# Longer runs of tile-sized matmuls in a decoder step's sparse attention: scores, values, pooling and compressed values

## The chip, the cores and the metric

The kernel runs on one core of a Trainium2 chip. The metric is the device time of one execution in microseconds (us); lower is better. Kernels are compared by the median of repeated runs on the same chip.

## The reference

One step of a one-layer hybrid decoder, for 256 prompt tokens and 8 sample sequences of 8 tokens (320 token rows in all), model width 2048, all in float32:

```python
h = rmsnorm(x); u = h @ w_in            # 2048 x 23664, columns shared out among the mixers
y = x + (sigmoid(m_A) * (GDN(u) @ w_branch_a) + sigmoid(m_B) * (NSA(u) @ w_branch_b)) @ w_out
```

GDN is a gated delta rule (32 heads of 128). NSA is sparse attention with 16 query heads over 4 key heads, and three branches that are added with gates:

- **compressed**: keys and values of 32 tokens, every 16 tokens, are pooled with learned weights and mapped by a 128x128 matrix; softmax over the 127 pooled blocks of a sequence, and a score that picks 16 blocks of 64 tokens.
- **selected**: attention over the picked blocks of the sequence's 2048 cached tokens (16 pages of 128 tokens, found through a page table), and the 8 new tokens. The kernel reads all 16 pages and masks what was not picked.
- **window**: attention over the last 512 cached tokens and the new ones.

The prompt has the same three branches over its own 256 tokens. Besides y, the step returns the new caches and states.

## The kernel before

The program is written out flat: Python code emits every instruction once, and each engine runs its list in that order. The order is not written by hand. The parts of the layer are generators ("streams"). Before each step a stream yields the engine it wants, and the buffers that have to be ready; `Run.go` takes the stream whose next step could start first by a planner (`Clock`, with assumed durations), lets it emit that step, and goes on. So what stands in the code as one step (between two yields) is emitted without other work in between; a yield is a place where other streams' work can come between. The projection (`p_load`, `p_hi`, `p_lo`, `p_mm`) has the lowest rank on TensorE and fills what the others leave.

**The projection.** `p_load` brings slabs of w_in (later w_branch_a, w_branch_b, w_out) of up to 1 MB into three buffers `wraw`. ScalarE rounds 128x512 pieces to `whi`, VectorE makes the remainder `wlo`, and TensorE multiplies each 128x128 block three times into `acc` (128x320): `hhi,whi`, `hlo,whi`, `hhi,wlo`. One 1 MB slab is 48 such matmuls, the whole layer 11,952 of them. Everything that the mixers need comes out of this, so the delta rule's work can only be reached in step with it.

**The attention streams**, which the change edits:

- `pooled` and `compressed` (lines 1158 to 1233): per sequence and per key or value, 16 pages of 128x512 through a `Feed` of 6 buffers `cpg`. Per step four pages are pooled by four matmuls with 32 weight columns each (`Pk`), which write partitions 0, 32, 64, 96 of `pp`. Then transposes, the 128x128 mapping, softmax, ranking (`select`).
- `scores` (line 1291): for each page, four 128x128 transposes into PSUM (`nt`), a copy to SBUF (`kT`, on ScalarE and VectorE in turn), and four matmuls of 32 columns, one per key head, into a quarter of `ns` each. `e.nt` pages go together: one in the window, two in the selected branch. The new tokens' scores (`kS`) follow at the end of each sequence as four 32x64 matmuls.
- `weighted` (line 1333): the softmax rows `x` are transposed four blocks at a time into `pT`, and each page of values gives four 32x128 matmuls into `op`, `e.nt` pages to a step; the new tokens' values (`vS`, 64 rows) are last.
- `prompt` (line 997): per key head and half of the tokens, four heads; the compressed probabilities are transposed as four 64-column blocks, and their values are a matmul with 64 rows (`vcp`) after the full ones in the same `op`.
- `window` runs beside `prompt` over the cached window with 5 page buffers `wpg`. When both are done, two `sample` workers (4 sequences each, 10 page buffers `spg` each) run the selected branch; the delta rule follows.

A float32 matmul is two matmuls in the trace (fp32 goes through twice); transposes and the fp32r matmuls of the projection are one. "Tile work" below means matmuls that use a part of the 128x128 array: 32 or 64 columns or rows. Pages go through the one queue of SyncE (SP), in the order of the program, with the weight slabs. For a page of `k_sel` or `v_sel` SP reads its number from a register; `page` (line 1129) keeps the numbers of a sequence in registers, and loads them again (`ptab`) when another sequence has taken the place.

Of the kernel before, what the change touches and what calls it, by code (L numbers as in the profile page):

```python
# [10 lines left out]
F32 = mybir.dt.float32  # L11
F32R = mybir.dt.float32r
I32 = mybir.dt.int32
AF = mybir.ActivationFunctionType
# [7 lines left out]
P = 128  # L22
# [20 lines left out]
NWP = 5  # L43
# [392 lines left out]
def step(ctx: ExitStack, tc: tile.TileContext, I, O):  # L436
# [395 lines left out]
    vcp = wtab.tile([64, 4, P], F32, name="vcp")  # L832
# [131 lines left out]
    def prompt_compress(tok):  # L964
        V.memset(kcpT, 0.0)
        V.memset(vcp, 0.0)
        for kv, nm in enumerate(("kc", "vc")):
            yield ("pe", tok[nm], Next(wps, "a"))
            pp = wps.tile([P, 512], F32, tag="a", name="pp")
            for t in range(2):  # L970
                T.matmul(pp[:32], Pk[:, kv, t], tok[nm][:, t], start=t == 0, stop=t == 1)
            yield "dve"
            pl = wk.tile([32, 512], F32, tag="wpcT", name="pl")
            V.tensor_tensor(pl.rearrange("p (g d) -> p g d", g=4), pp[:32].rearrange("p (g d) -> p g d", g=4),
                            bc(cb[:32, kv], [[0, 4], [1, P]]), op=OP.add)
            yield ("pe", clock.last, Next(wps, "b"))
            tp = wps.tile([P, 512], F32, tag="b", name="tp")
            for g in range(4):
                T.transpose(tp[:, g * 32:g * 32 + 32], pl[:, g * P:g * P + P], ident[:32, :32])
            yield "dve"  # L980
            pt = wprep.tile([P, P], F32, tag="pt", name="pt")
            V.tensor_copy(pt, tp[:, :P])
            yield ("pe", clock.last, Next(wps, "b"))
            if kv == 0:
                kp = wps.tile([P, 512], F32, tag="b", name="kp")
                T.matmul(kp[:, :P], proj[:, 0], pt, start=True, stop=True)
                rs = yield from rstd(wprep, wps, "a", kp[:, :P], P, None)
                V.scalar_tensor_tensor(kcpT[:, :, :32], kp[:, :P].rearrange("p (g n) -> p g n", g=4), gains[:, 1:2],
                                       rs.rearrange("p (g n) -> p g n", g=4), op0=OP.mult, op1=OP.mult)
            else:  # L990
                vp = wps.tile([P, 512], F32, tag="b", name="vp")
                for g in range(4):
                    T.matmul(vp[:32, g * P:g * P + P], pt[:, g * 32:g * 32 + 32], proj[:, 1], start=True, stop=True)
                yield "dve"
                V.tensor_copy(vcp[:32].rearrange("p g d -> p (g d)"), vp[:32])

    def prompt():
        yield lambda: done["names"]
        qp = {}
        for g, tt in ((g, tt) for g in range(4) for tt in range(2)):  # L1000
# [35 lines left out]
            pcT = wk.tile([64, 512], F32, tag="wpcT", name="pcT")  # L1036
            S.activation(pcT, tp[:64], AF.Copy)
            ob = wk.tile([P, 4, P], F32, tag="wob", name="ob")
            for h in range(4):
# [38 lines left out]
                T.matmul(op[:, :P], vcp[:, g], pcT[:, h * P:h * P + P], start=False, stop=True)  # L1078
# [73 lines left out]
    cfeed = Feed(cp, "cpg", 6, [page(key, b, 4 * j + i) for b in range(B) for key in ("k_cmp", "v_cmp")  # L1152
                                for i in range(4) for j in range(4)], CR)

    def qT(b, g):
        return qs[:, b, 4 * g:4 * g + 4, :].rearrange("p h t -> p (h t)")

    def pooled(b, kv):
        pp = cps.tile([P, 512], F32, tag="a", name="pp")
        for i in range(4):  # L1160
            pg = []
            for _ in range(4):
                pg.append((yield from cfeed.get()))
            yield ("pe", *pg)
            for j in range(4):
# [4 lines left out]
            cfeed.release(4)  # L1170
# [66 lines left out]
    def select(h):  # L1237
# [17 lines left out]
        for a in (0, 15):  # L1255
            big = cp.tile([P, 2, 450], F32, tag="big", name="big", bufs=1)
            mine, other = bc(sc[:, a:], [[1, 15], [0, 30]]), bc(sc, [[0, 15], [1, 30]])
            v = [big[:, k].rearrange("p (a b) -> p a b", a=15) for k in range(2)]
# [13 lines left out]
    class Env:  # L1272


        def __init__(self, pp, st, tt, nt, pl, n, i, feed):
            self.feed, self.next, self.nt = feed, Next(pp, tt), nt
            self.s = lambda name: pp.tile([P, 512], F32, tag=st, name=name)
            self.t = lambda name: pp.tile([P, 512], F32, tag=tt, name=name, bufs=nt)
            self.x = lambda name: pl.tile([P, 512], F32, tag=f"{name}{i}", name=name, bufs=n)
# [11 lines left out]
    def scores(e, b, npg, dst, kS, finish):  # L1291

        for quad in range(0, npg, 4):
            ns = e.s("ns")
            prev = []
            for p in range(0, 4 + e.nt, e.nt):
                got, now = [], []
                if p < 4:
                    for _ in range(e.nt):
                        got.append((yield from e.feed.get()))  # L1300
                    yield ("pe", *got, e.next)
                    for k, pg in enumerate(got):
                        if k:
                            yield ("pe", e.next)
                        nt = e.t("nt")
                        for g in range(4):
                            T.transpose(nt[:, g * P:g * P + P], pg[:, g * P:g * P + P], ident)
                        now.append(nt)
                        e.feed.release()
                if prev:  # L1310
                    yield ("pe", *prev)
                    for k, kT in enumerate(prev):
                        for g in range(4):
                            T.matmul(ns[32 * g:32 * g + 32, (p - e.nt + k) * P:(p - e.nt + k + 1) * P], qT(b, g), kT[:, g * P:g * P + P], start=True, stop=True)
                prev = []
                for k, nt in enumerate(now):
                    prev.append(e.x("kT"))
                    if (p + k) % 2:
                        yield ("dve", nt)
                        V.tensor_copy(prev[k], nt)  # L1320
                    else:
                        yield ("act", nt)
                        S.activation(prev[k], nt, AF.Copy)
            yield ("dve", ns)
            finish(quad, ns)
        yield ("pe",)
        ns = e.s("ns")
        for g in range(4):
            T.matmul(ns[32 * g:32 * g + 32, :64], qT(b, g), kS[:, g], start=True, stop=True)
        yield "dve"  # L1330
        V.scalar_tensor_tensor(dst[:, npg * P:npg * P + 64], ns[:, :64], SCALE, newB[:, 56 - 8 * b:120 - 8 * b], op0=OP.mult, op1=OP.add)

    def weighted(e, b, npg, x, vS, op):
        prev = None
        for quad in list(range(0, npg + 1, 4)) + [None]:
# [8 lines left out]
            if prev is not None:  # L1344
                q0, n0, m0, pT = prev
                for k in range(0, n0, e.nt):
                    got = []
                    for _ in range(min(e.nt, n0 - k)):
                        got.append((yield from e.feed.get()) if q0 < npg else vS)
                    yield ("pe", *got, pT)  # L1350
                    for i, pg in enumerate(got):
                        c = (k + i) * P
                        for g in range(4):
                            T.matmul(op[32 * g:32 * g + 32], pT[:m0, c + 32 * g:c + 32 * g + 32], pg[:m0, g * P:g * P + P],
                                     start=q0 == 0 and k + i == 0, stop=q0 == npg)
                        if q0 < npg:
                            e.feed.release()
            if quad is not None:
                pT = e.x("pT")
# [6 lines left out]
                prev = quad, n, m, pT  # L1366

    def window():
        for b in range(B):
# [7 lines left out]
            yield from scores(wenv, b, 4, xw, kwS, fin_w)  # L1377
            yield from softmax(xw, 576, b, 2, mx)
            op = wenv.s("op")
# [20 lines left out]
    wenv = Env(wps, "a", "b", 1, wwin, 1, "", Feed(wwin, "wpg", NWP, [wpage(key, b, p) for b in range(B) for key in ("k_win", "v_win") for p in range(4)]))  # L1400
# [8 lines left out]
    def sample(smp, sps, n, bs):  # L1409
        req = [page(key, b, p) for b in bs for key in ("k_sel", "v_sel") for p in range(16)]  # L1410
        env = Env(sps, "s", "t", 2, smp, 2, "", Feed(smp, "spg", n, req))
        for b in bs:
# [16 lines left out]
            yield from scores(env, b, 16, xs, ksS, fin_s)  # L1429
# [3 lines left out]
            op = sps.tile([P, 512], F32, tag="s", name="op")  # L1433
# [905 lines left out]
```

## Time and profile before

| | |
|---|---|
| median of 3 runs | 2661.42 us (2658.48 to 2663.15) |
| the profiled execution's own time | 2657.93 us |
| its span, first to last instruction | 2655.9 us |
| TensorE matmul busy | 2581.8 us (97%), 22228 instructions |
| TensorE weight load busy | 2332.5 us (88%) |
| VectorE, ScalarE, GpSimd busy | 62%, 53%, 15% |
| HBM traffic over the span | 203 GB/s |
| mean granted TensorE clock | 0.988 |

What lies around the span is 2.0 us. In the profile PE is TensorE's matmuls and PEld its weight loads, DVE is VectorE, ACT ScalarE, POOL GpSimd, SPq the queue of SyncE. A row of the timeline gives the start, the time from the first start to the last end, and how many equal matmuls were merged. Matmuls overlap, so the distance from one start to the next is what a matmul costs, not its duration. All operations go through one recording helper, so the line is L330 nearly everywhere and the tile names tell them apart: `acc` is the projection, `pp` pooling, `nt` a transpose of a page or of softmax rows, `ns` scores, `op` values, `ps`, `pu` and `bank` the delta rule.

In time the program is: norms and the first weights, pooling beside the projection (84 to 858 us), prompt and window (438 to 811 us), the selected branch (818 to 1107 us), the delta rule's state beside the projection (1322 to 2222 us), and the projections out to the end.

### The profile page before, as it was taken

To read this page: it belongs to the slowest core of one execution; us is meant where nothing else is said; L and a number is where in the kernel's file an instruction comes from. 1 tells how busy PE (TensorE), PEld (TensorE's weight loads), DVE (VectorE), ACT (ScalarE), POOL (GpSimd) and SP (SyncE) were. 2 spreads that over 40 slices of the span, in tenths; PEclk is the share of its full clock that TensorE was granted. 3 is DMA by queue.
4 is the path that set the end of the run, shared out by engine and by line. 5 is a ranking of instruction groups with operands and counts; after the bars stand their busy time and mean duration, and the time that the engine had idled before them with its cause. 6 is when DMAs were issued, how large, how long until landed. Compare 5 with 4: busy or idle time off the path is not lost. (4 is left out here: it accounts for less than half of the span.)

```text
span 2655.9 us, 59457 instructions
## 1 busy us (share of the span) xinstructions
PE 2581.8 (97%) x22228; PEld 2332.5 (88%) x22228; DVE 1648.4 (62%) x4089; ACT 1407.7 (53%) x3290; POOL 398.0 (15%) x967
## 2 busy tenths in 40 slices
PE   7999999999999999999999899989999899999999
PEld 5897788777878888899999699979998789999999
DVE  5554445655556555544887787878878776454543
ACT  5453443434433333345778568777777565444443
POOL 2000011000000000000222343324242322000000
PEclk9999999999999999999999899989999899999999
DMA  6747777898768998765546256545464366656654
GB/s 193 232 156 242 232 238 268 273 322 267 252 207 281 316 359 273 242 195 156 153 152 189 88 179 180 163 131 154 145 189 147 122 195 216 208 180 191 184 191 131
DMA packets 548677, 543.89 MB, mean 205 GB/s; under 512 B 32482, under 2 KB 452499, under 8 KB 548003
## 3 DMA queue, kind: packets, MB, share of 16 engines
q1 hardware_dynamic: 534308, 493.67, 58.3%
q0 software_dynamic: 14080, 46.41, 5.1%
q8 instruction: 175, 2.87, 0.4%
q14 instruction: 114, 0.93, 0.1%
HBM read 470.31 MB, written 69.67 MB: 203 GB/s over the span
## 5 line engine op out<-in xcount | busy, mean ns | idle before, releaser
L330 PE MATMUL acc<-hhi,whi 128*128 128x320 f32 (+1 forms) x3472 | 1146.3, 330 | 1.5 <-ACT hhi L330 1.5
L330 PE MATMUL acc<-hhi,wlo 128*128 128x320 f32 (+1 forms) x3472 | 1075.3, 310 | 0.0
L330 PE MATMUL acc<-hlo,whi 128*128 128x320 f32 (+1 forms) x3472 | 1074.1, 309 | 0.5 <-DVE hlo L330 0.4
L330 ACT ACTIVATE whi<-wraw 128x512 fp32r<-128x512 f32 (+1 forms) x996 | 626.2, 630 | 834.5 <-PE acc L330 792.4
L330 DVE TENSOR_TENSOR wlo<-wraw,whi 128x512 fp32r<-128x512 f32 x992 | 685.4, 694 | 576.3 <-ACT whi L330 545.6
L330 PEld LDWEIGHTS acc<-hhi,whi 128*128 128x128 f32 (+1 forms) x3472 | 654.9, 189 | 70.1 <-issue 57.4
L330 PEld LDWEIGHTS acc<-hlo,whi 128*128 128x128 f32 (+1 forms) x3472 | 655.6, 189 | 7.0 <-issue 2.2
L330 PEld LDWEIGHTS acc<-hhi,wlo 128*128 128x128 f32 (+1 forms) x3472 | 653.5, 188 | 0.0
L330 PE MATMUL acc<-oah,whi 128*128 128x320 f32 x512 | 158.2, 309 | 0.0
L330 PE MATMUL acc<-oal,whi 128*128 128x320 f32 x512 | 158.2, 309 | 0.0
L330 PE MATMUL acc<-oah,wlo 128*128 128x320 f32 x512 | 158.2, 309 | 0.0
L330 POOL CAST vx<-v 32x128 fp32r<-32x128 f32 x256 | 97.8, 382 | 143.7 <-DVE v L330 91.5
L298 POOL DMA_DIRECT2D d_mz<-raw x48 | 26.2, 545 | 605.5 <-ACT raw L330 594.1
L330 DVE SCALAR_TENSOR_TENSOR cv<-xp,cw,cv 128x344 f32<-128x344 f32 x192 | 109.9, 573 | 6.0 <-ACT cv L330 4.7
L330 ACT ACTIVATE kT<-nt 128x512 f32<-128x512 f32 x80 | 47.6, 596 | 109.2 <-PE ns L330 63.4
L330 DVE COPY kT<-nt 128x512 f32<-128x512 f32 x80 | 55.1, 690 | 69.7 <-PE ns L330 51.6
L330 PEld LDWEIGHTS acc<-oah,whi 128*128 128x128 f32 x512 | 96.1, 188 | 0.0
L330 PEld LDWEIGHTS acc<-oal,whi 128*128 128x128 f32 x512 | 96.1, 188 | 0.0
L330 PEld LDWEIGHTS acc<-oah,wlo 128*128 128x128 f32 x512 | 96.1, 188 | 0.0
L330 DVE SCALAR_TENSOR_TENSOR sS<-sS,ends,pu 128x128 f32<-128x128 f32 x256 | 82.8, 338 | 19.0 <-PE pu L330 18.1
L330 PE MATMUL pp<-cpg,Pk 128*32 128x512 f32 x608 | 88.0, 602 | 0.8 <-DMA cpg<-cache_k_cmp 0.7
L330 PE MATMUL nt<-pk_const,spg 128*128 128x128 f32 x512 | 68.5, 275 | 1.2 <-DVE kT L330 0.9
(422 smaller groups left out, 3436.3 us busy)
## 6 DMA issues: line engine op xcount, KB each, us to landing
wraw<-w_in SPq DMA_DIRECT2D x136, 1024.0 KB
wraw<-w_in SPq DMA_DIRECT2D x97, 512.0 KB
cpg<-cache_k_cmp SPq DMA_DIRECT2D x128, 256.0 KB
cpg<-cache_v_cmp SPq DMA_DIRECT2D x128, 256.0 KB
spg<-cache_k_sel SPq DMA_DIRECT2D x128, 256.0 KB
spg<-cache_v_sel SPq DMA_DIRECT2D x128, 256.0 KB
wraw<-w_branch_a SPq DMA_DIRECT2D x32, 1024.0 KB
sS<-state_gdn SPq DMA_DIRECT2D x32, 512.0 KB
```

The costliest lines, as they stand in the source:

```text
L298: return f(*a, **k)
L330: return f(*a, **k)
```

## The change

Six edits, all in the attention. Sums and results stay the same.

1. **Pooling** takes eight pages a step (two of the four groups) instead of four; `cpg` has 8 buffers, not 6.
2. **Scores**: each page is a step of its own for the transposes and the copy, and the score matmuls of `nk` pages go together at the end: 2 pages in the window, 4 in the selected branch (with 4 buffers `kT`, not 2).
3. **New tokens' scores** are made ahead (`new_scores`): in the selected branch for all four sequences of a worker at once, into `xn`, from where GpSimd copies them to the softmax row of each sequence.
4. **Values**: four pages a step (all of a `quad`), and the new tokens' values go first, in the step of the first four pages, not last on their own. The window has 4 page buffers, not 5.
5. **The prompt's compressed values**: the probabilities of two heads are transposed together (two 128-column blocks for four 64-column ones), and `vcp` holds the values twice, at partitions 0 and 64 with zeros elsewhere, so that the value matmul has 128 rows like its neighbours.
6. The prompt's queries `qp` have one buffer, not two, and are loaded when the last group has been read; `select` uses two existing buffers for its scratch.

```diff
-NWP = 5
+NWP = 4
...
-    vcp = wtab.tile([64, 4, P], F32, name="vcp")
+    vcp = wtab.tile([P, 2, 4, P], F32, name="vcp")
...
-                for x in range(len(qp), min(g + 2, 4)):
-                    yield ("sp",)
-                    qp[x] = wwin.tile([P, 4, TP], F32, tag="qp", name="qp", bufs=2)
-                    SY.dma_start(qp[x], d_q[x])
+                yield ("sp", Next(wwin, "qp"))
+                qp[g] = wwin.tile([P, 4, TP], F32, tag="qp", name="qp")
+                SY.dma_start(qp[g], d_q[g])
...
-            for h in range(4):
-                T.transpose(tp[:64, h * P:h * P + P], pc[:, h], ident)
+            for h in range(2):
+                T.transpose(tp[:, h * P:h * P + P], pc[:, 2 * h:2 * h + 2].rearrange("p h n -> p (h n)"), ident)
...
-                T.matmul(op[:, :P], vcp[:, g], pcT[:, h * P:h * P + P], start=False, stop=True)
+                T.matmul(op[:, :P], vcp[:, h % 2, g], pcT[:, h // 2 * P:h // 2 * P + P], start=False, stop=True)
...
-        for i in range(4):
+        for i in range(0, 4, 2):
             pg = []
-            for _ in range(4):
+            for _ in range(8):
                 pg.append((yield from cfeed.get()))
             yield ("pe", *pg)
-            for j in range(4):
-                T.matmul(pp[32 * j:32 * j + 32], Pk[:, kv, i], pg[j], start=i == 0, stop=i == 3)
+            for k in range(8):
+                j = k % 4
+                T.matmul(pp[32 * j:32 * j + 32], Pk[:, kv, i + k // 4], pg[k], start=i + k // 4 == 0, stop=i + k // 4 == 3)
...
+    def scores(e, b, npg, finish):
 
         for quad in range(0, npg, 4):
+            ks, ns = [], None
+            for p in range(4):
+                pg = yield from e.feed.get()
+                yield ("pe", pg, e.next)
+                nt = e.t("nt")
+                for g in range(4):
+                    T.transpose(nt[:, g * P:g * P + P], pg[:, g * P:g * P + P], ident)
+                e.feed.release()
+                ks.append(e.x("kT", e.nk))
...
+                if len(ks) < e.nk:
+                    continue
+                yield ("pe", *ks, *([] if ns else [e.sum]))
+                ns = ns or e.s("ns")
+                for k, kT in enumerate(ks, p + 1 - e.nk):
+                    for g in range(4):
+                        T.matmul(ns[32 * g:32 * g + 32, k * P:k * P + P], qT(b, g), kT[:, g * P:g * P + P], start=True, stop=True)
+                ks = []
...
-        for quad in list(range(0, npg + 1, 4)) + [None]:
+        for quad in [npg] + list(range(0, npg, 4)) + [None]:
...
+            if quad not in (0, npg):
+                got = []
+                for q0, n0, m0, pT in pend:
+                    for k in range(n0):
+                        got.append(((yield from e.feed.get()) if q0 < npg else vS, pT, k, m0))
+                last = quad is None
+                yield ("pe", *[y[0] for y in got], *[y[3] for y in pend])
...
+        xn = smp.tile([P, len(bs), 64], F32, name="xn")
+        yield from new_scores(env, bs, ksS, xn)
...
+            yield ("pool", xn, Place(clock, xs))
+            G_.tensor_copy(xs[:, 2048:], xn[:, i])
```

Since the planner sets the order, the edits move far more rows than they name. Two places on TensorE, both in the selected branch. First the scores of one worker (`nt<-pk_const,spg`: transposes of key pages; `ns<-kT,qs`: score matmuls, four to a page; the order counts an fp32 matmul once). Before:

```order
L330 MATMUL nt<-pk_const,spg 128x128 x4
L330 MATMUL acc<-hhi,whi 128x320
L330 MATMUL acc<-hlo,whi 128x320
L330 MATMUL acc<-hhi,wlo 128x320
L330 MATMUL nt<-pk_const,spg 128x128 x4
L330 MATMUL ns<-kT,qs 32x128 x8
L330 MATMUL acc<-hhi,whi 128x320
```

After:

```order
L330 MATMUL acc<-hhi,wlo 128x320
L330 MATMUL ns<-kT,qs 32x128 x16
L330 MATMUL acc<-hhi,whi 128x320
L330 MATMUL acc<-hlo,whi 128x320
L330 MATMUL acc<-hhi,wlo 128x320
L330 MATMUL nt<-pk_const,spg 128x128 x4
```

The scores of two pages were one run of eight; those of four pages are one run of sixteen. The transposes now come a page at a time between pieces of the projection.

Second the values (`nt<-pk_const,xs`: transposes of softmax rows; `op<-spg,pT`: value matmuls, four to a page; `op<-vsS,pTn`: the new tokens' values). Before:

```order
L330 MATMUL nt<-pk_const,xs 128x128 x4
L330 MATMUL op<-spg,pT 32x128 x16
L330 MATMUL nt<-pk_const,xs 128x128 x4
L330 MATMUL op<-spg,pT 32x128 x8
L330 MATMUL nt<-pk_const,spg 128x128 x8
```

After:

```order
L330 MATMUL nt<-pk_const,xs 128x128 x4
L330 MATMUL op<-vsS,pTn 32x128 x4
L330 MATMUL op<-spg,pT 32x128 x16
L330 MATMUL nt<-pk_const,xs 128x128 x4
L330 MATMUL op<-spg,pT 32x128 x32
```

Runs of eight (two pages) are gone; every run has four pages or more, and the new tokens' values stand directly ahead of the first pages.

Counted over the whole order, with the 64-column transposes taken as full-array work: the stretches in which TensorE does tile work between full-array work go from 422 to 284. 126 of them, in the delta rule, are the same in both. Of the others, those that are followed by a matmul of the projection go from 188 to 87, those followed by other full-array work from 108 to 71. The matmuls of the projection ahead of the selected branch's first page go from 3264 to 3624, and ahead of its last page from 4008 to 4509; from the 4707th matmul of the projection on, TensorE's order is the same to the end (the delta rule's first state matmul, `pu`, stands behind 5337 of them in both). On SP the loads of page numbers (`ptab`) go from 34 to 56.

More of the change, by code (lines that the diff above doesn't have):

```diff
@@ L991, in prompt_compress @@
                 vp = wps.tile([P, 512], F32, tag="b", name="vp")
-                for g in range(4):
-                    T.matmul(vp[:32, g * P:g * P + P], pt[:, g * 32:g * 32 + 32], proj[:, 1], start=True, stop=True)
+                for i in range(2):
+                    for g in range(4):
+                        T.matmul(vp[64 * i:64 * i + 32, g * P:g * P + P], pt[:, g * 32:g * 32 + 32], proj[:, 1], start=True, stop=True)
                 yield "dve"
-                V.tensor_copy(vcp[:32].rearrange("p g d -> p (g d)"), vp[:32])
+                for i in range(2):
+                    V.tensor_copy(vcp[64 * i:64 * i + 32, i].rearrange("p g d -> p (g d)"), vp[64 * i:64 * i + 32])
     def prompt():
@@ L1150, in wpage @@
         return f
-    cfeed = Feed(cp, "cpg", 6, [page(key, b, 4 * j + i) for b in range(B) for key in ("k_cmp", "v_cmp")
+    cfeed = Feed(cp, "cpg", 8, [page(key, b, 4 * j + i) for b in range(B) for key in ("k_cmp", "v_cmp")
                                 for i in range(4) for j in range(4)], CR)
@@ L1255, in select @@
         for a in (0, 15):
-            big = cp.tile([P, 2, 450], F32, tag="big", name="big", bufs=1)
+            big = [cp.tile([P, 450], F32, tag=t, name="big", bufs=1) for t in ("c2", "c3")]
             mine, other = bc(sc[:, a:], [[1, 15], [0, 30]]), bc(sc, [[0, 15], [1, 30]])
-            v = [big[:, k].rearrange("p (a b) -> p a b", a=15) for k in range(2)]
+            v = [x.rearrange("p (a b) -> p a b", a=15) for x in big]
             yield "dve"
@@ L1272, in step, with __init__ @@
     class Env:
-        def __init__(self, pp, st, tt, nt, pl, n, i, feed):
-            self.feed, self.next, self.nt = feed, Next(pp, tt), nt
+        def __init__(self, pp, st, tt, nt, pl, nk, feed):
+            self.feed, self.next, self.sum, self.nk = feed, Next(pp, tt), Next(pp, st), nk
             self.s = lambda name: pp.tile([P, 512], F32, tag=st, name=name)
             self.t = lambda name: pp.tile([P, 512], F32, tag=tt, name=name, bufs=nt)
-            self.x = lambda name: pl.tile([P, 512], F32, tag=f"{name}{i}", name=name, bufs=n)
+            self.new = lambda name: pl.tile([64, P], F32, tag=name, name=name)
+            self.x = lambda name, n: pl.tile([P, 512], F32, tag=name, name=name, bufs=n)
     def softmax(x, n, b, br, mx):
@@ L1289, in softmax @@
         V.tensor_tensor(mx[:, 2:3], mx[:, 1:2], gS[:, br, b:b + 1], op=OP.mult)
-    def scores(e, b, npg, dst, kS, finish):
-        for quad in range(0, npg, 4):
[L1294 to L1323, printed above, removed]
@@ new lines, in new_scores @@
+    def new_scores(e, bs, kS, dst):
+        yield ("pe", e.sum)
+        ns = e.s("ns")
+        for i, b in enumerate(bs):
+            for g in range(4):
+                T.matmul(ns[32 * g:32 * g + 32, 64 * i:64 * i + 64], qT(b, g), kS[:, g], start=True, stop=True)
+        for i, b in enumerate(bs):
+            yield ("dve", ns)
+            V.scalar_tensor_tensor(dst[:, i], ns[:, 64 * i:64 * i + 64], SCALE, newB[:, 56 - 8 * b:120 - 8 * b], op0=OP.mult, op1=OP.add)
+    def scores(e, b, npg, finish):
+        for quad in range(0, npg, 4):
+            ks, ns = [], None
[3 more added lines that the diff above has]
+                nt = e.t("nt")
+                for g in range(4):
+                    T.transpose(nt[:, g * P:g * P + P], pg[:, g * P:g * P + P], ident)
+                e.feed.release()
+                ks.append(e.x("kT", e.nk))
+                if p % 2:
+                    yield ("dve", nt)
+                    V.tensor_copy(ks[-1], nt)
+                else:
+                    yield ("act", nt)
+                    S.activation(ks[-1], nt, AF.Copy)
+                if len(ks) < e.nk:
[3 more added lines that the diff above has]
+                for k, kT in enumerate(ks, p + 1 - e.nk):
+                    for g in range(4):
+                        T.matmul(ns[32 * g:32 * g + 32, k * P:k * P + P], qT(b, g), kT[:, g * P:g * P + P], start=True, stop=True)
+                ks = []
@@ L1324, in scores @@
             yield ("dve", ns)
             finish(quad, ns)
[L1326 to L1331, printed above, removed]
     def weighted(e, b, npg, x, vS, op):
-        prev = None
-        for quad in list(range(0, npg + 1, 4)) + [None]:
+        pend = []
@@ L1343, in weighted @@
                     T.transpose(nt[:m, k * P:k * P + P], x[:, c:c + m], ident)
[L1344 to L1357, printed above, removed]
+            if quad not in (0, npg):
[5 more added lines that the diff above has]
+                yield ("pe", *[y[0] for y in got], *[y[3] for y in pend])
+                for i, (pg, pT, k, m0) in enumerate(got):
+                    for g in range(4):
+                        T.matmul(op[32 * g:32 * g + 32], pT[:m0, k * P + 32 * g:k * P + 32 * g + 32], pg[:m0, g * P:g * P + P],
+                                 start=pg is vS, stop=last and i == len(got) - 1)
+                e.feed.release(sum(y[0] is not vS for y in got))
+                pend = []
             if quad is not None:
-                pT = e.x("pT")
+                pT = e.x("pT", 2 if npg > 4 else 1) if quad < npg else e.new("pTn")
                 if quad // 4 % 2:
@@ L1365, in weighted @@
                     S.activation(pT[:m, :n * P], nt[:m, :n * P], AF.Copy)
-                prev = quad, n, m, pT
+                pend.append((quad, n, m, pT))
     def window():
@@ L1375, in fin_w @@
                 V.scalar_tensor_tensor(xw[:, :8], ns[:, :8], SCALE, winB, op0=OP.mult, op1=OP.add)
-            yield from scores(wenv, b, 4, xw, kwS, fin_w)
+            yield from new_scores(wenv, (b,), kwS, xw[:, 512:].rearrange("p (a k) -> p a k", a=1))
+            yield from scores(wenv, b, 4, fin_w)
             yield from softmax(xw, 576, b, 2, mx)
+            yield ("pe", wenv.sum)
             op = wenv.s("op")
@@ L1399, in step @@
     wwin = pool(w_ctx, "wwin")
-    wenv = Env(wps, "a", "b", 1, wwin, 1, "", Feed(wwin, "wpg", NWP, [wpage(key, b, p) for b in range(B) for key in ("k_win", "v_win") for p in range(4)]))
+    wenv = Env(wps, "a", "b", 1, wwin, 2, Feed(wwin, "wpg", NWP, [wpage(key, b, p) for b in range(B) for key in ("k_win", "v_win") for p in range(4)]))
     run.add(window())
@@ L1432, in sample @@
             yield from softmax(xs, 2112, b, 1, mx)
-            op = sps.tile([P, 512], F32, tag="s", name="op")
+            yield ("pe", env.sum)
+            op = env.s("op")
             yield from weighted(env, b, 16, xs, vsS, op[:, 0:P])
```

13 lines of the change are left out of this document (7 added, 6 removed).

## Prediction

> **What bounds the kernel now.** I read the page's busy times first, then busy time by stage, the waits, and the end of the chain.
>
> ```profile
> PE 2581.8 (97%) x22228; PEld 2332.5 (88%) x22228; DVE 1648.4 (62%) x4089; ACT 1407.7 (53%) x3290; POOL 398.0 (15%) x967
> ```
>
> ```profile
> core 0: us, PE busy (x) PEld busy (x) DVE busy (x) ACT busy (x) POOL busy (x), PEclk, DMA share, GB/s
> 440.00:815.00 375.00, 373.60 (x2993) 296.66 (x2992) 217.11 (x598) 153.23 (x369) 19.60 (x33) 1.00 0.77 260
> 815.00:1105.00 290.00, 286.04 (x3626) 237.01 (x3624) 158.60 (x275) 109.19 (x183) 8.65 (x16) 1.00 0.90 309
> 1319.00:2220.00 901.00, 853.24 (x8276) 800.54 (x8276) 709.03 (x2121) 638.87 (x1762) 295.20 (x767) 0.97 0.51 155
> ```
>
> ```profile
> ACT whi L330 <- PE acc L330: 792.4, 687, 5.0
> ...
> PE ns L330 <- DVE xs L330: 1.7, 7, 0.3
> ...
> PE ns L330 <- DVE xw L330: 1.2, 3, 0.5
> ```
>
> ```profile
> 2228.98 312.40 PE acc L330 x2130
> ```
>
> In prompt and window (second row) and the selected branch (third) TensorE stands still for 1.4 and 4.0 us, at the full granted clock. ScalarE, which makes the weight pieces, waits 792 us for TensorE to give a buffer back: the supply is ahead. At the end TensorE runs 312 us without a gap. So each us that TensorE saves in the attention should come off the end, if nothing new makes it wait. Only the delta rule's stage has real idle time (48 of 901 us); its order on TensorE is the same in both kernels, and it is tied to the projection's progress (first `pu` behind matmul 5337), so I carry it over as it is.
>
> **The change part by part.** What it removes is the way in and out of tile work. First the plain steps, from starts in the timeline:
>
> ```profile
> 834.68 1.03 PE L330 MATMUL nt<-pk_const,spg 128*128 128x128 f32 x8
> 835.47 0.39 PE L330 MATMUL acc<-hhi,whi 128*128 128x320 f32 x1
> 835.70 0.30 PE L330 MATMUL acc<-hlo,whi 128*128 128x320 f32 x1
> ...
> 850.23 0.31 PE L330 MATMUL acc<-hhi,whi 128*128 128x320 f32 x1
> ...
> 853.16 0.31 PE L330 MATMUL acc<-hhi,wlo 128*128 128x320 f32 x1
> ```
>
> Between the last two rows lie 20 steps of the projection in 2.93 us: 0.147 us each. From eight transposes to the second projection matmul is 1.02 us; less one step, 0.109 us per transpose. Nothing is left over: breaking the projection with full-array work costs nothing, so edit 2's scattered single-page transposes are priced at zero. Next, tile work:
>
> ```profile
> 845.16 0.31 PE L330 MATMUL acc<-hhi,wlo 128*128 128x320 f32 x1
> 845.40 0.64 PE L330 MATMUL ns<-kT,qs 128*32 128x128 f32 x16
> 845.97 0.42 PE L330 MATMUL acc<-hhi,whi 128*128 128x320 f32 x1
> 846.23 0.31 PE L330 MATMUL acc<-hlo,whi 128*128 128x320 f32 x1
> ...
> 856.76 1.08 PE L330 MATMUL op<-spg,pT 128*32 128x128 f32 x32
> 857.65 1.04 PE L330 MATMUL pp<-cpg,Pk 128*32 128x512 f32 x8
> 858.63 0.66 PE L330 MATMUL nt<-pk_const,xs 128*128 128x128 f32 x4
> 859.21 0.65 PE L330 MATMUL op<-spg,pT 128*32 128x128 f32 x16
> 859.79 0.66 PE L330 MATMUL tp<-pk_const,pl 128*128 128x128 f32 x4
> ```
>
> From `op` x32 (four pages) to `pp`, both 32 columns wide, nothing changes size: 0.89 us, 0.22 us a page. Now the stretch at 845.40 (two pages): from 845.16 to 846.23 are 1.07 us; two projection steps (0.29) and two pages (0.44) leave 0.335 us, the price of one stretch of tile work that returns to the projection, however long it is. The one at 859.21 returns to transposes: from 858.63 to 859.79 are 1.16 us; four transposes (0.44) and two pages (0.44) leave 0.28 us.
>
> Of the 0.335, 0.09 is the way in (845.16 to 845.40 against 0.147), and 0.11 the late second projection matmul (0.26 against 0.147).
>
> - **Fewer stretches** (edits 1 to 5). By the order 101 stretches less return to the projection and 37 less to other full-array work: 101 x 0.335 + 37 x 0.28 = 33.8 + 10.4 = 44.2 us.
> - **Compressed values of the prompt** (edit 5). Their 32 stretches are among those; they have a slow second pass besides:
>
> ```profile
> 449.69 0.39 PE L330 MATMUL op<-pT,tok_vw 128*128 128x128 f32 x2
> 450.01 0.48 PE L330 MATMUL op<-pcT,vcp 64*128 64x128 f32 x2
> 450.42 0.41 PE L330 MATMUL acc<-hhi,whi 128*128 128x320 f32 x1
> 450.68 0.31 PE L330 MATMUL acc<-hlo,whi 128*128 128x320 f32 x1
> ```
>
>   0.99 us for four passes and one projection step; at full size 4 x 0.109 + 0.147 = 0.58. The 0.41 is 0.07 over the price of a stretch: 32 x 0.07 = 2.2 us. Half of the 32 transposes go: 16 x 0.109 = 1.7 us. The second copy of the values costs 4 small matmuls once, and VectorE a larger memset and a copy: under 1 us, beside the projection.
> - **New tokens' scores** (edit 3): TensorE waited 1.7 and 1.2 us ahead of them for VectorE to read the last scores from the same PSUM buffer; made ahead, this goes: 2.9 us. GpSimd's copy of 128x64 to the softmax row is needed only by the reduction that follows all pages, and GpSimd is busy for 8.65 of 290 us there.
> - **One `qp` buffer** (edit 6): three loads can no longer run ahead of the prompt stream. That delays the stream, not TensorE: the projection fills. Cover: the selected branch now ends behind projection matmul 4509, the first `pu` behind 5337; 828 x 0.147 = 122 us lie between.
> - **New waits.** Steps that want four or eight pages at once, give them back together, and the page numbers that SP loads 22 times more:
>
> ```profile
>   DMA cpg<-cache_k_cmp: 5.6, 9
>   DMA cpg<-cache_v_cmp: 1.4, 3
> ...
> L1138 SPq TENSOR_LOAD <-ptab x34: 967/974/1457, 79.2 to 1054.7; - x34
> ```
>
> ```profile
>   DMA spg<-cache_v_sel: 2.3, 6
>   DMA spg<-cache_k_sel: 0.7, 3
> ```
>
>   Matmuls and weight loads now wait 7.0 and 3.0 us for pages. Bounds: 10 us better if all of it goes, 22 x 0.974 = 21 us worse if every additional load of numbers holds a page that TensorE waits for, with the weight slabs queued behind it on SP. I take 5 us worse, nearer to today's rows: SP's queue is filled ahead of need, and buffers for eight and twenty pages remain.
>
> Sum: 44.2 + 2.2 + 1.7 + 2.9 - 5 = 46 us. The profiled execution took 2657.9 us (2655.9 of span, 2.0 around it), so it would take 2612; it lies 3.5 us under the median of the runs shown, 2661.4, and on that scale the forecast is 2615 us.
>
> **The rivals.**
>
> *B: batches wait.* The order has 32 pooling steps of eight pages and 40 value steps of four pages (8 in the window, 32 in the selected branch). Today's waits for `cpg` are 7.0 us in 12: 0.58 each. If half of the 72 wait so, 21 us instead of my 5: 2631 us; all of them, 2652. For it: in the window four buffers serve a step that takes all four, and a buffer must be written out before it is filled. Against: the order puts projection work ahead of most of those steps.
>
> *E: only the change of size goes.* The way in and out may be worth less to a long run than to a short one, if the late start behind it is part of the tile work itself. Then a stretch saves two ways of 0.09 us: 138 x 0.18 = 25 us instead of 44, and the kernel takes 2634 us. Against it: 0.335 was the remainder after whole pages were taken out, and 0.22 a page holds inside a run of four. [...]
>
> *C: TensorE is not the bound.* [...] The mechanism would be that the chain from slab to `wlo` sets the pace, and TensorE only waits longer for pieces: no change, 2661 us. Against it: the 792 us that ScalarE waits for TensorE, and steps of 0.147 us without a gap.
>
> *D: the selected branch becomes bound by its pages (slower).*
>
> ```profile
> spg<-cache_k_sel SPq DMA_DIRECT2D x128, 256.0 KB
> ```
>
> ```profile
> 900.00:1000.00 100.00, 99.12 (x1397) 80.19 (x1385) 52.99 (x93) 37.87 (x65) 2.16 (x4) 1.00 1.00 351
> 1000.00:1100.00 100.00, 99.32 (x1215) 85.20 (x1217) 52.33 (x88) 39.37 (x67) 3.78 (x7) 1.00 0.79 259
> ```
>
> The stage moves 256 pages of 256 KB (67 MB) and, with 885 projection matmuls now between its first and last page (744 before) at 48 per MB, 19 MB of weights: 86 MB. TensorE needs about 289 us for it: 290, plus 141 x 0.147 = 21, less 55 stretches (42 x 0.335 + 13 x 0.28 = 18) and the pooling that has moved ahead (4). At the 351 GB/s of the first row the transfers take 246 us and hide. At the 259 of the second, cut by the share of SP's time that 22 more number loads take (at least 21 of 289 us), 240 GB/s, they take 360: 71 us of waiting, 2615 + 71 = 2686 us. It decides below 86 / (289 + 46) = 257 GB/s. Against it: the 259 came with TensorE busy for 99 of 100 us, so it was what was asked for, not what was to be had.
>
> **How the numbers follow.** Chances: forecast 0.73, B 0.12, E 0.05, C 0.04, D 0.06. The range goes from 2605 us (with all page waits gone the sum gives 2600; two thirds of the way) to 2638 us (B with two thirds of its steps waiting; E lies inside), and leaves out C, D and the worst of B. A measurement of this kernel can tell about 0.2%, 5 us, from no change. Faster by more: forecast, B and E, 0.90. Within: C, 0.04. Slower: 0.06, from D.
>
> **What would show it.** In the changed profile: matmul busy near the span as before, the same 0.335 us around stretches at 32 columns, `op<-pcT,vcp` as 128 rows with steps of 0.11 us, no wait of `ns` for `xs` or `xw`; the selected branch ending later than 1107 us, but the first `pu` near 1275 us, not 1322, and everything behind it shifted by the same amount. Waits of PE and PEld for `spg`, `cpg`, `wpg` of 15 us and more together would speak for B; a selected branch with a DMA share of 0.9 and more throughout and TensorE idle for tens of us for D; ScalarE no longer waiting for `acc`, and TensorE waiting for `whi` or `wlo`, for C. [...]

## The result, and the profile after

| | before | after |
|---|---|---|
| median | 2661.19 us (2658.48 to 2663.15, 4 runs) | 2618.06 us (2612.48 to 2621.82, 4 runs) |
| ratio | | 0.9837 (95%: 0.9817 to 0.9857) |
| the profiled execution | 2657.93 us | 2618.77 us |
| its span | 2655.9 us | 2616.7 us |
| granted TensorE clock, mean | 0.988 | 0.985 |

The changed kernel is 43 us faster; 46 were forecast, and 2615 us as its time. The page's busy line:

```profile
PE 2535.8 (97%) x22220; PEld 2337.6 (89%) x22220; DVE 1648.8 (63%) x4090; ACT 1402.9 (54%) x3290; POOL 399.6 (15%) x975
```

Matmul busy time fell by 46.0 us and the span by 39.2, with eight instructions less of 22228: it is the same sums in fewer pieces. 7 us of the saving became standing time (74.1 us in the span before, 80.9 after). Busy time by stage (prompt and window, selected branch, delta rule), then the chain's long piece at the end:

```profile
440.00:815.00 375.00, 375.00 (x3189) 326.62 (x3188) 232.41 (x622) 161.30 (x383) 21.57 (x37) 1.00 0.82 275
815.00:1105.00 290.00, 283.66 (x3569) 258.40 (x3567) 157.20 (x271) 115.05 (x203) 12.95 (x28) 0.99 0.89 296
1280.00:2180.00 900.00, 852.28 (x8259) 800.05 (x8257) 707.16 (x2113) 637.70 (x1758) 294.03 (x763) 0.96 0.51 155
```

```profile
2189.75 312.40 PE acc L330 x2130
```

In prompt and window TensorE has no idle time left and does 3189 matmuls where it did 2993. In the stretch from 815 to 1105 us it stands still for 6.3 us (4.0 before), and the granted clock is no longer full: that is new. The delta rule's 900 us keep their 48 us of idle time. The end is the same 312.40 us, 39.2 us earlier; the first `pu` stands at 1280.8 us (1321.6 before). So the gain was made, and part of it lost again, ahead of the delta rule's state. A joined score step of four pages, and the compressed values, in the timeline:

```profile
456.89 0.39 PE L330 MATMUL op<-pT,tok_vw 128*128 128x128 f32 x2
457.12 0.39 PE L330 MATMUL op<-pcT,vcp 128*128 128x128 f32 x2
457.34 0.60 PE L330 MATMUL nt<-pk_const,wpg 128*128 128x128 f32 x4
...
914.00 0.31 PE L330 MATMUL acc<-hhi,wlo 128*128 128x320 f32 x1
914.24 1.08 PE L330 MATMUL ns<-kT,qs 128*32 128x128 f32 x32
915.25 0.41 PE L330 MATMUL acc<-hhi,whi 128*128 128x320 f32 x1
915.50 0.31 PE L330 MATMUL acc<-hlo,whi 128*128 128x320 f32 x1
```

From 914.00 to 915.50 are 1.50 us: two projection steps (0.29) and four pages (0.88) leave 0.33, the price that a stretch of two pages had. `vcp` now has 128 rows and its steps are 0.11 us like its neighbours'. What waits, first all engines, then TensorE's own new rows:

```profile
ACT whi L330 <- PE acc L330: 808.8, 677, 7.8
...
PE bank L330 <- DMA pk_gini<-c_gini: 3.5, 1, 3.5
...
PE nt L330 <- DMA spg<-cache_k_sel: 2.6, 3, 1.3
...
PE mp L330 <- DVE xn L330: 2.4, 1, 2.4
...
PE bank L330 <- DMA c<-gdn_conv_w: 1.2, 1, 1.2
```

Pages, with the matmuls' and the weight loads' waits together (us, times):

```profile
  DMA cpg<-cache_k_cmp: 2.2, 5
  DMA cpg<-cache_v_cmp: 1.0, 2
...
  DMA spg<-cache_k_sel: 4.5, 6
  DMA spg<-cache_v_sel: 3.5, 5
```

ScalarE still waits for TensorE (808.8 us), and the waits of `ns` for `xs` and `xw` are gone. Waits for pages are 11.2 us (10.0 before). But two waits are new that have nothing to do with pages: `mp` for `xn`, 2.4 us where the selected branch begins, and `bank` for two small loads, 4.7 us where the delta rule begins. Both are followed by something else. Busy time and granted clock around them (the column ahead of the DMA share is the clock):

```profile
840.50:843.20 2.70, 0.31 (x3) 0.29 (x2) 1.05 (x8) 0.54 (x1) 0.47 (x2) 1.00 0.03 9
843.40:846.80 3.40, 3.40 (x13) 3.00 (x14) 1.39 (x5) 0.00 (x0) 0.00 (x0) 0.50 0.92 268
846.80:850.00 3.20, 3.20 (x27) 3.17 (x27) 1.38 (x2) 1.74 (x3) 0.00 (x0) 1.00 0.98 325
...
1151.50:1155.70 4.20, 0.43 (x4) 0.33 (x4) 0.00 (x0) 0.00 (x0) 0.00 (x0) 0.80 0.72 256
1155.70:1160.80 5.10, 5.09 (x19) 4.98 (x20) 1.68 (x5) 0.75 (x2) 0.00 (x0) 0.50 1.16 313
```

After the gap TensorE is busy, but at half the clock: for 3.4 us behind the first gap (13 matmuls where the next 3.2 us hold 27), for 6.8 us from 1154.0 us on, within the second. In the first slow stretch a step of the projection takes 0.267 us in place of 0.147. So the two gaps cost 7.1 us of standing and, by my estimate, about 4 us of slow running (1 - 0.147 / 0.267 = 0.45, of 3.4 and of 5.1 us). What they wait for is in the timeline, of VectorE and TensorE and then of SP's queue, TensorE's row last:

```profile
842.15 1.14 DVE L330 SCALAR_TENSOR_TENSOR xn<-ns,newB 128x64 f32<-128x64 f32 x8 [3.31 <-DMA d_ob<-ob]
...
842.91 0.37 PE L330 MATMUL mp<-selm,pk_nsa 32*128 32x32 f32 x2 [2.39 <-DVE xn L330]
...
1145.69 1.00 SPq L298 DMA_DIRECT2D wraw<-w_in  x2
1146.92 0.98 SPq L298 DMA_DIRECT2D c<-gdn_conv_w  x1
...
1150.01 0.46 SPq L298 DMA_DIRECT2D pk_gini<-c_gini  x1
...
1155.71 0.69 PE L330 MATMUL bank<-bag,pk_gini 64*128 64x64 f32 x2 [3.51 <-DMA pk_gini<-c_gini]
```

VectorE writes `xn` only when `ob` has been sent out, and `mp` on TensorE waits for VectorE to be done with `xn`. The delta rule's constants are issued behind a weight slab, and TensorE is there before they land: `c` is issued at 1146.92 us and TensorE is free at 1150.6, 3.7 us later. In the kernel before, 8.4 us lay between (1116.25 and 1124.62), and nothing waited.

A sum over the whole trace puts a size on both sides. I took each group of equal matmuls in a row, from its first start to the first start of the next group, and as its free price the median of the groups of the same length between the same neighbours in nine kernels of this study, without those that hold a wait over 0.15 us or run at less than the full clock (where none was left, with the neighbours matched less closely). (Single steps are no measure here: inside the changed kernel's run of pooling matmuls at 541.27 us four start within 0.02 us, and the next four come 0.41 to 0.43 us behind them.) In the kernel before, free groups make 2543.6 us, and the rest, waiting and slow clock, 96.1. After, they make 2496.3 and 104.2. So work fell by 47.3 us, and waiting grew by 8.1: together the 39 us by which the profiled span fell. Other ways of matching the groups move these differences by up to 4 us, and those of single edits below by up to 2.5.

### The profile page after: what moved, and what is told of

Read it like the earlier page. It is cut to its first block, busy times and chain, and to the rows that moved or that the text cites. A ratio compares the mean times of both kernels' runs of the same rounds, so it can differ in the third digit from the quotient of the medians.

```text
span 2616.7 us, 59450 instructions
## 1 busy us (share of the span) xinstructions
PE 2535.8 (97%) x22220; PEld 2337.6 (89%) x22220; DVE 1648.8 (63%) x4090; ACT 1402.9 (54%) x3290; POOL 399.6 (15%) x975
## 5 line engine op out<-in xcount | busy, mean ns | idle before, releaser
L330 ACT ACTIVATE whi<-wraw 128x512 fp32r<-128x512 f32 (+1 forms) x996 | 626.5, 630 | 868.4 <-PE acc L330 808.8
L330 PEld LDWEIGHTS acc<-oah,whi 128*128 128x128 f32 x512 | 96.1, 188 | 0.0
L330 PEld LDWEIGHTS acc<-oal,whi 128*128 128x128 f32 x512 | 96.1, 188 | 0.0
L330 PEld LDWEIGHTS acc<-oah,wlo 128*128 128x128 f32 x512 | 96.1, 188 | 0.0
L330 DVE SCALAR_TENSOR_TENSOR sS<-sS,ends,pu 128x128 f32<-128x128 f32 x256 | 82.8, 338 | 18.5 <-PE pu L330 17.6
L330 PE MATMUL pp<-cpg,Pk 128*32 128x512 f32 x608 | 77.9, 598 | 0.0
L330 PE MATMUL nt<-pk_const,spg 128*128 128x128 f32 x512 | 75.3, 274 | 2.6 <-DMA spg<-cache_k_sel 2.6
```

The lines of the kernel that those rows point to most:

```text
L330: return f(*a, **k)
```

## The experiments

My theory: each stretch of tile work costs about 0.335 us whatever its length, TensorE is the bound, and new waits took the rest. Rivals: E (a long stretch saves only the change of size), B and D (batches wait, or the branch is bound by pages), and that some of the edits brought nothing.

### The price of a stretch, by itself

To the changed kernel 1024 matmuls with 32 columns were added, late in the program, where no attention work is left (the stage of w_branch_a). They write a PSUM bank of their own, and nobody reads the result. The same 1024 come as 256 stretches of four (`s_many`), 64 of 16 (`s_four`) or 16 of 64 (`s_long`); `s_full` has 1024 full-size transposes in 256 groups instead.

```
+ if q["kt"] == 32 and k % 2 == 0:       # s_four: k % 8 == 6, range(4); s_long: k % 32 == 30, range(16)
+     for _ in range(1):
+         for j in range(4):
+             T.matmul(pj["scr"][32*j:32*j+32, :P], ident[:, 32*j:32*j+32], ident, start=True, stop=True)
```

> The changed kernel with 1024 additional 32-column matmuls (128x128 moving, results unused) between projection matmuls of the w_branch_a stage, as 256 stretches of four. If a stretch costs 0.335 us whatever its length, and four matmuls 0.22 us: 256 x 0.555 = 142 us more, 2760 us. If only the two changes of size count (E, 0.18 us): 256 x 0.40 = 102 us, 2720 us. If TensorE is not the bound there (C): no change, 2618 us.

> The same 1024 additional matmuls as 64 stretches of sixteen. Price per stretch 0.335 us: 64 x (0.335 + 0.88) = 78 us more, 2696 us, so 64 us less than in 256 stretches. E: 64 x (0.18 + 0.88) = 68 us, 2686 us, 34 us less than in 256 stretches. C: 2618 us.

> The same 1024 additional matmuls as 16 stretches of sixty-four. Price per stretch 0.335 us: 16 x (0.335 + 3.52) = 62 us more, 2680 us; from 256 stretches to 16 is then 80 us. E: 16 x (0.18 + 3.52) = 59 us, 2677 us, and 43 us from 256 to 16. C: 2618 us.

> At the same 256 places four full-array 128x128 transposes in place of the four 32-column matmuls. If breaking the projection with full-array work is free: 256 x 4 x 0.109 = 112 us more, 2730 us, with 0.44 us at each place. If every break costs (a late second projection matmul of 0.1 us): 26 us more than that, 2756 us. C: 2618 us.

Measured: 2758.98, 2695.11, 2675.55 and 2729.0 us, beside 2658.09 for the kernel before (ratios 1.0381, 1.0343 to 1.0419; 1.0141, 1.0103 to 1.0178; 1.0075, 1.0052 to 1.0098; 1.0268, 1.0226 to 1.0311). Between the first and the third lie 83.4 us for 240 stretches: 0.348 us each, where E allowed 43 us in all. (`s_four` against `s_many`: 63.9 us for 192 stretches, 0.333 each.) The timelines of `s_many` and then of `s_long` show it at one stretch each:

```profile
2299.73 0.31 PE L330 MATMUL acc<-oah,wlo 128*128 128x320 f32 x1
2299.97 0.43 PE L330 MATMUL scr<-pk_const 128*32 128x128 f32 x8
2300.32 0.41 PE L330 MATMUL acc<-oah,whi 128*128 128x320 f32 x1
2300.57 0.31 PE L330 MATMUL acc<-oal,whi 128*128 128x320 f32 x1
```

```profile
2277.20 0.31 PE L330 MATMUL acc<-oah,wlo 128*128 128x320 f32 x1
2277.44 3.70 PE L330 MATMUL scr<-pk_const 128*32 128x128 f32 x128
2281.07 0.41 PE L330 MATMUL acc<-oah,whi 128*128 128x320 f32 x1
2281.33 0.30 PE L330 MATMUL acc<-oal,whi 128*128 128x320 f32 x1
```

0.84 and 4.13 us from the first row to the last; without two projection steps 0.546 and 3.836. The difference is 60 matmuls, so one is 0.055 us, and 0.546 less four of them leaves 0.327 us: the price, the same for 4 and for 64. A stretch of 64 starts its projection as late (0.26 us to the second matmul) as one of four. `s_full` took 111 us more than the changed kernel, 0.108 per transpose: full-size work between projection matmuls cost only itself here. And what was added moved the end by about its own steps (`s_many`: 56 us of matmuls and 256 x 0.335 make 142, measured 141; `s_long`: 62, measured 57), so TensorE is the bound.

### Each edit undone alone

From the changed kernel, one edit at a time goes back: pooling of four pages a step (`u_pool`), compressed values with 64 rows (`u_vc`), scores of one page in the window and two in the selected branch (`u_scores`), values of two pages a step (`u_vals`).

```
u_pool:   - for i in range(0, 4, 2):                 u_vc:   - vcp = wtab.tile([P, 2, 4, P], F32, name="vcp")
          -     for _ in range(8):                           + vcp = wtab.tile([64, 4, P], F32, name="vcp")
          + for i in range(4):                               ...
          +     for _ in range(4):                           - T.matmul(op[:, :P], vcp[:, h % 2, g], ...)
          ...                                                + T.matmul(op[:, :P], vcp[:, g], ...)
u_scores: - wenv = Env(..., wwin, 2, ...)            u_vals: - for i, (pg, pT, k, m0) in enumerate(got):
          + wenv = Env(..., wwin, 1, ...)                    + while todo:    # two pages a step; new tokens' with the first
          - env = Env(..., smp, 4, ...)                      +     now, todo = todo[:2 + ...], todo[2 + ...:]
          + env = Env(..., smp, 2, ...)                      ...
```

> The changed kernel with pooling of four pages a step again (eight buffers stay). By the order 26 stretches more, 13 back to the projection and 13 to other full-array work: 13 x 0.335 + 13 x 0.28 = 8 us slower than the changed kernel, 2626 us. If batches of eight pages cost waits (B), part of that comes back: 2618 to 2623 us. E (0.18 us a stretch): 2623 us.

> The changed kernel with the prompt's compressed values at 64 rows again. 25 stretches more (16 and 9), the slow second pass 32 times, 16 transposes: 5.4 + 2.5 + 2.2 + 1.7 = 12 us slower, 2630 us. It changes no page batches, so B says the same. E: 4.5 + 2.2 + 1.7 = 8 us, 2626 us.

> The changed kernel with scores of one page a run in the window and two in the selected branch again. 40 stretches more, all back to other full-array work: 40 x 0.28 = 11 us slower, 2629 us. E: 7 us, 2625 us. B says the same as the forecast, since the pages come one by one in both.

> The changed kernel with values two pages a step again (the new tokens' values still first). 17 stretches more (3 and 14): 1.0 + 3.9 = 5 us slower, 2623 us. If the batches of four pages cost waits (B), it is no slower or even faster, down to 2610 us. E: 2621 us.

| undone | median us | ratio to before (95%) | counted price | free work in the trace |
|---|---|---|---|---|
| `u_pool` | 2617.49 | 0.9854 (0.9832 to 0.9876) | 13 x 0.335 + 13 x 0.28 = 8.0 | +7.2 |
| `u_vc` | 2629.76 | 0.9894 (0.9876 to 0.9911) | 16 x 0.335 + 9 x 0.28 + 2.2 + 1.7 = 11.8 | +10.8 |
| `u_scores` | 2630.31 | 0.9896 (0.9879 to 0.9913) | 40 x 0.28 = 11.2 | +10.7 |
| `u_vals` | 2624.80 | 0.9870 (0.9852 to 0.9889) | 3 x 0.335 + 14 x 0.28 = 4.9 | +3.5 |

The last column is the sum of free groups less the changed kernel's, worked out as above. In work, all four edits are worth what the count of their stretches says, to 1.5 us. In time, three are worth 12, 12 and 7 us. (Times are against 2618.06 us and, measured again below, 2617.52 for the changed kernel, which did not run beside these four. The 7 us of the values are not clear of noise: the interval of `u_vals` overlaps those of the changed kernel.) For the values B falls all the same, by which smaller steps would have waited less: waiting is 110.2 us in `u_vals` and 104.2 in the changed kernel. Pooling of eight is the exception: its work is there, but no time at all. B's forecast for `u_pool`, 2618 to 2623 us, came nearer than my 2626. Yet steps of eight do not wait longer for their own pages: for `cpg` the changed kernel waits 3.2 us, `u_pool` 4.3. The profiled execution of `u_pool`, 2612.61 us and the fastest of its four, has no wait of `bank` for `pk_gini` or `c` in it, and waiting in all is 13.0 us less than in the changed kernel's: other steps have moved too. So the boundary waits have to go first, before pooling can be judged.

### Where the waiting comes from

`f_wait` moves two steps in the planner's order: the new tokens' scores of the selected branch come due later, so that VectorE need not wait in `mp`'s way, and the delta rule's first `bank` step comes due 16 us behind its loads. `fw_pool` is `f_wait` with pooling of four pages. `f_all` is `f_wait` with page numbers kept per worker: a sequence's numbers are dropped only when the same worker takes its next sequence. `again` is the changed kernel itself. The kernel before took 2658.49 us beside them.

```
f_wait:  + yield ("pe", (clock.t["pe"] + 6000, "sp"))        # ahead of new_scores, in sample
         - yield ("pe", clock.last, Place(clock, bank[:, :384]))
         + yield ("pe", (clock.t["sp"] + 16000, "sp"), Place(clock, bank[:, :384]))
fw_pool: the same, and u_pool's edit
f_all:   the same, and
         - x[1] % 2 == b % 2
         + (x[1] in SW[0][1]) == (b in SW[0][1])
```

> The changed kernel itself, as the neighbour of the next three: 2618 us, within 5.

> The changed kernel with two steps put later, behind more projection work: the first new-token scores of each worker (6 us of planned time) and the delta rule's first matmuls (at least 16 us after their loads are issued). If the two waits there (2.4 us for xn, 4.7 us for the first tables) and the half clock that follows each (10 us at half, 5 us lost) are what the changed kernel lost: 11 to 12 us faster, less 1 us for 4 stretches more, 2607 us. If such waits only move (another step waits in their place): 2618 us.

> The kernel of f_wait with pooling of four pages a step. By the order 16 stretches more (11 back to the projection, 5 to other work): 11 x 0.335 + 5 x 0.28 = 5 us slower than f_wait, 2612 us. If joined pooling is worth nothing, as the first attempt seemed to say, because batches of eight wait: the same as f_wait, 2607 us.

> The kernel of f_wait with the page numbers kept per worker, so that SP loads them 16 times, not 56. If loads of numbers hold pages that TensorE waits for (the sharp end of D): the 4 us of waits for spg go, 2603 us. If SP's queue is far enough ahead: the same as f_wait, 2607 us.

| | median us | ratio to before (95%) |
|---|---|---|
| `again` | 2617.52 | 0.9852 (0.9838 to 0.9865) |
| `f_wait` | 2612.03 | 0.9826 (0.9813 to 0.9839) |
| `fw_pool` | 2604.30 | 0.9802 (0.9788 to 0.9816) |
| `f_all` | 2601.97 | 0.9794 (0.9781 to 0.9808) |

In `f_wait` both waits are gone from the list, and 5 us from the time, half of the 11 forecast (the intervals just touch). One reason is that the first wait has only moved, as the rival had it. Where the selected branch begins, TensorE now stands 2.2 us for its first pages instead of `xn`, and the granted clock from 850 to 900 us is 0.97, by my estimate from that mean some 3 us at half (the first row has the longest wait last, the second the clock ahead of the DMA share):

```profile
PE nt L330 <- DMA spg<-cache_k_sel: 4.5, 5, 2.2
...
850.00:900.00 50.00, 49.86 (x691) 44.09 (x692) 29.09 (x45) 21.29 (x35) 1.08 (x2) 0.97 0.97 351
```

`f_all` has the same gap (2.3 us) and the same 0.97; `fw_pool` has neither (1.0 us at most, and 1.00). `fw_pool` is where my count fails outright as a forecast of time: 16 stretches more than `f_wait`, and 8 us faster. Pages, in `f_wait`:

```profile
  DMA spg<-cache_v_sel: 7.4, 10
  DMA spg<-cache_k_sel: 7.4, 7
```

In `fw_pool`:

```profile
  DMA spg<-cache_k_sel: 1.0, 1
  DMA spg<-cache_v_sel: 0.4, 2
```

In `f_all`:

```profile
  DMA spg<-cache_k_sel: 4.8, 2
```

And the stretch from 1000 to 1150 us, in `f_wait`, `fw_pool` and `f_all`:

```profile
1000.00:1150.00 150.00, 144.59 (x1755) 129.57 (x1754) 78.74 (x133) 57.12 (x100) 6.35 (x13) 1.00 0.89 292
```

```profile
1000.00:1150.00 150.00, 148.97 (x1789) 137.78 (x1782) 80.07 (x135) 59.93 (x104) 7.26 (x14) 1.00 0.91 297
```

```profile
1000.00:1150.00 150.00, 150.00 (x1797) 138.06 (x1790) 80.76 (x137) 60.44 (x104) 6.97 (x14) 1.00 0.86 279
```

In `f_wait` the selected branch asked for its pages sooner than they came: 5.4 us of idle time in the last part of the stage, against 1.0 and none. The DMA engines were not full (0.89, against 1.01 in the changed kernel from 850 to 900 us). What holds the pages is tried in `f_all`, which takes away most of SP's loads of page numbers; in `f_wait` and then in `f_all`:

```profile
L1139 SPq TENSOR_LOAD <-ptab x58: 966/976/1645, 76.5 to 1054.8; - x58
```

```profile
L1139 SPq TENSOR_LOAD <-ptab x16: 969/998/1807, 76.1 to 1037.5; - x16
```

42 loads of 0.976 us are 41 us of SP's queue, through which all pages and slabs go. Without them waits for `spg` fall from 14.8 to 4.8 us, which are the one gap at the stage's start, counted for the matmul and for its weight load, and the time falls by 10.1 us, outside the intervals. That the loads alone did it is not shown: the planner counts them too, so TensorE's order differs between the two from 926 to 1175 us, and `fw_pool`, with 56 loads, hardly waits for pages. `f_all` is the fastest version of the study, 56.5 us under the kernel before.

That pooling of four does nearly as well is explained in part. A step of pooling costs what the others cost; in `f_wait` (16 pooling matmuls in a step) and then `fw_pool` (8):

```profile
537.80 0.31 PE L330 MATMUL acc<-hhi,wlo 128*128 128x320 f32 x1
538.04 1.92 PE L330 MATMUL pp<-cpg,Pk 128*32 128x512 f32 x16
539.90 0.42 PE L330 MATMUL acc<-hhi,whi 128*128 128x320 f32 x1
540.15 0.31 PE L330 MATMUL acc<-hlo,whi 128*128 128x320 f32 x1
```

```profile
542.96 0.31 PE L330 MATMUL acc<-hhi,wlo 128*128 128x320 f32 x1
543.20 1.06 PE L330 MATMUL pp<-cpg,Pk 128*32 128x512 f32 x8
544.19 0.41 PE L330 MATMUL acc<-hhi,whi 128*128 128x320 f32 x1
544.44 0.30 PE L330 MATMUL acc<-hlo,whi 128*128 128x320 f32 x1
```

2.35 and 1.48 us: two of the second, less 0.29 for the projection steps that come twice, are 0.32 more than one of the first. So a joined pair saves a stretch, and over the whole program free work differs by 4.9 us, the 5 of the count. Against it stand 18.5 us less of waiting and slow clock in `fw_pool`'s trace. 6.4 us of them are standing time ahead of the delta rule's state, as much as TensorE's matmuls wait less for `spg` (7.4 us in `f_wait`, 1.0 in `fw_pool`). About 6 us, an estimate as above, are slow clock within the delta rule, where the order of both is the same. The medians are only 7.7 us apart, not the 13.6 of these two traces, since `f_wait`'s is its slowest execution (2615.9 us). That the larger batch itself causes the `spg` waits is not shown: it also shifts when every later step runs, and no run changed one without the other.

## Why the prediction was right

- **The bound.** Right, and shown both ways: 57 to 141 us of added work moved the end by about its own size, and of 47.3 us of work less 39 came off the profiled span, the rest lost to waits. C falls with it (ScalarE still waits 809 us). The busy share of TensorE's weight loads went up, from 88 to 89%, while the time fell.
- **The price of a stretch.** Right: 0.335 forecast, 0.327 at one stretch and 0.348 over 240, without regard to length. E falls: 25 us where the same stretches brought some 43 (47.3 less 2.2 and 1.7).
- **The number of stretches.** Right for all four edits, undone one by one, to 1.5 us of work each. In all, work was to fall by 48.1 us (44.2 + 2.2 + 1.7) and fell by 47.3. That pooling's share of it shows as no time is a matter of waits.
- **Waits that go.** Right: `ns` waits for neither `xs` nor `xw`, 2.9 us.
- **New waits: mis-sized.** The term was 5 us; with the 2.9 that went, a net rise of 8.1 makes it 11.0. For pages, which the term was made of, it was too careful: 11.2 us against 10.0. What it lacked was the two stage boundaries, 7.1 us of standing. The new buffer `xn` must wait for `ob` to be sent out; and the delta rule's loads, which nothing in the change touches, were issued 3.7 us ahead of their use, not 8.4. Both gaps are also followed by half the clock for a while, about 4 us, which I had not priced at all. That the term still had the right sign and half the size is luck: what it was made of hardly came.
- **D** did not happen: the branch ran at 0.89 of the DMA engines with 6 us of idle time. Its sharp end, SP's number loads in the way of pages, may be real at a small size: 42 loads fewer came with 10 us less in `f_all`, in another order of TensorE's steps.
- The two misses (0.8 us of work, 6.0 of waits) add up to the 7 us by which the profiled execution missed its sum of 2612. The medians are nearer, 3 us.

## What to carry to other kernels

Where tile-sized matmuls break up a stream of full-size ones on a TensorE that is the bound, price each break from starts in the timeline (here a third of a microsecond, whatever the length), count the breaks in both orders, and the work that is saved follows to within two microseconds. Then look where the faster engine will arrive early, above all at stage boundaries and first uses of new buffers, since a short gap can be followed by a slower clock (here 2.39 us of standing by 3.4 us at 0.50, an estimated 1.5 us more). A batch that makes its engine's work shorter can still be worth nothing, because every later step moves with it; undo each part alone before keeping it.

## What the runs showed of the hardware

- Behind two short standstills of TensorE the granted clock was 0.50. In the changed kernel the gap of 2.39 us ahead of `mp` was followed by 3.4 us at 0.50; in that of 3.51 us ahead of `bank` (with 1.19 us shortly before) 6.8 us at 0.50 began. `fw_pool`, whose longest wait in the attention is 1.0 us, has a clock of 1.00 from 80 to 1290 us. The length of the longest gap alone does not decide: in the changed kernel 1.09 us ahead of 2137.98 us (with 0.86 and 0.64 us shortly behind) were followed by 3.4 us at 0.50 from 2140.5 us on, and 1.56 us ahead of 1505.42 us left the clock at 1.00 until 1734 us. The slow stretches begin on a grid as long as the shortest of them: in the kernel before and in the changed one their starts lie whole multiples of 3.413 us apart, the two above 310.6 us, 91 times that. Why some gaps are followed by half the clock and others not was not shown.
- Joining tile work of equal form showed no cost of its own: in `s_long` a stretch of 64 matmuls goes in and out as a stretch of four does in `s_many` (0.327 us for either).
- The 0.335 us of a stretch of 32-column matmuls lie at four places in its starts. In the changed kernel's score step at 914.24 us the first start comes 0.09 us late, the second four start 0.02 us later than the steps of 0.11 us inside, the projection starts 0.11 us late behind the last four, and its second matmul 0.11 us late again.
